# Operand pairs of reused weights stored to HBM at their first use and loaded at their second

## The chip, the cores and the metric

The kernel runs on one core of one Trainium2 chip, in one launch. The metric is the device time of one execution in microseconds; three runs of the kernel before gave 1142.05, 1142.27 and 1142.57, median 1142.27. The engines are TensorE (PE in the profile, its weight loads PEld), VectorE (DVE), ScalarE (ACT), GpSimd (POOL) and SyncE (SP), which issues all of this kernel's DMA transfers on one queue (SPq), in a fixed order.

## The reference

One layer on 1024 tokens of width 1024, float32. In the cut below, `u @ w_in` is the input projection (1024 x 2568), `mix @ w_out` the output projection (1024 x 1024); between them lie a pooling group (p) and a gated delta rule over chunks with q, k, v, z.

```python
u = rms_norm(h, norm_mix[l])
proj = u @ w_in[l]
pool_out = pool_mixer(proj[..., :P], w_pool[l], pool_scale[l])
qkv = causal_conv_silu(proj[..., P:P + 3 * G], conv_w[l])
z = proj[..., P + 3 * G:P + 4 * G]
...
gdn_out = gated_delta_net(qkv[..., :G], qkv[..., G:2 * G], qkv[..., 2 * G:], z, a, b, ...)
mix = jnp.concatenate([pool_out, gdn_out], axis=-1)
h = h + mix @ w_out[l]
u = rms_norm(h, norm_mlp[l])
h = h + jnp.square(jax.nn.relu(u @ w_up[l])) @ w_down[l]
return rms_norm(h, norm_final)
```

## The kernel before

**Pairs.** Matrix products keep float32 accuracy by splitting each operand into a rounded part (hi, type float32r) and the rest (lo) and adding three products: hi x hi, hi x lo, lo x hi (`mm3`, `mm3_steps`). `split_w` makes a weight's pair: SyncE loads the raw block into one of three `raw` buffers (line 128), ScalarE casts it to hi (line 132), and VectorE or GpSimd subtracts to get lo (line 133). The pairs live in the pool `ws` under the tags `wh` and `wl`, five buffers each: a sixth pair waits until the first one's last matmul is through.

**Input projection.** The 1024 tokens are taken as two halves of 512 (i = 0 and 1). `project(i, what, eng)` makes 512 output columns for one half in two blocks of 256 columns; `in_weights(col, eng)` makes a block's four pairs of [128, 2, 256] (256 KB a part). A block is 48 matmuls: first pairs 0 and 1 for both groups of 128 columns, then pairs 2 and 3 for both. The first half goes k, q, v, z, p; the second k, q, v, p, z. So each of the ten blocks of weights is loaded and split twice, once for each half. `eng`, which subtracts, is GpSimd for k of the first half and VectorE for the rest of it, and GpSimd for all of the second half.

**Strands.** Between the matmuls of the projections run the steps of the delta rule (`prepare`, `query`, `invert`, `correct`, `scan`), the gates, the convolutions and the pooling, as generators. `dense()` and `run()` put TensorE's instructions in one order, worked out from TensorE's own assumed rate, and this order is kept as written. The order on the other engines and on SyncE's queue is made by a scheduler from its own simulated times, with earlier lines of the program first among what is ready; only in part of the MLP is VectorE's and ScalarE's order written out too.

**Output projection.** `wout_weights(n, ks)` makes the eight pairs of [128, 512] for columns half n; pairs 4 to 7 lie in a pool `wo`, which opens where the projection's inputs u were. `out_proj(t, n, wt, ...)` adds one tile of 128 tokens: 24 matmuls over the eight pairs in order k = 0 to 7. Tiles 0 to 3 take both halves; tiles 4 to 7 first take half 1, and then, after the recurrence has ended and the MLP's inputs for the first tokens have been transposed (`turn_first`), half 0, for which the eight pairs of half 0 are loaded and split a second time (lines 880 and 881), pairs 4 to 7 with raw buffers of their own (pool `w2`).

**MLP.** Up and down projection follow from about 475 us on. Nothing in them is touched.

Of the kernel before, what the change touches and what calls it, by code (L numbers as in the profile page):

```python
# [8 lines left out]
F32 = mybir.dt.float32  # L9
F32R = mybir.dt.float32r  # L10
# [5 lines left out]
P = 128  # L16
# [3 lines left out]
KT = D // P  # L20
NT = S // P
NH = 4
HALF = 512
# [5 lines left out]
def hybrid_trunk(ctx, tc, x, norm_mix, w_in, conv_w, w_pool, pool_scale, a_log, dt_bias,  # L29
                 gdn_norm, w_out, norm_mlp, w_up, w_down, norm_final, out):  # L30
    nc = tc.nc
    V, A, G, T = nc.vector, nc.scalar, nc.gpsimd, nc.tensor
# [23 lines left out]
    def opened(**kw):  # L56
        c = tc.tile_pool(**kw)
        return c, c.__enter__()

    def close(c):  # L60
        c.__exit__(None, None, None)

    const = ctx.enter_context(tc.tile_pool(name="const", bufs=1))
    ws = ctx.enter_context(tc.tile_pool(name="ws", bufs=2))
# [6 lines left out]
    def big_tile(nm, shape, dt=F32):  # L71
        return big.tile([P] + shape, dt, name=nm, tag="big")
# [4 lines left out]
    def load_x(i):  # L77
        xin[i] = []
        for j in range(2):
            t = big_tile("xin", [2, D])  # L80
            for e in range(2):
                r0 = (CH * i + 2 * j + e) * P
                nc.sync.dma_start(out=t[:, e, :], in_=x2[r0:r0 + P, :])
            xin[i].append(t)
# [40 lines left out]
    def split_w(src, shape, eng, hp=None, ht="wh", lt="wl", bufs=5, rp=None, rbufs=3):  # L125

        raw = (rp or ws).tile(shape, F32, name="raw", tag="raw", bufs=rbufs)
        last["load"] = nc.sync.dma_start(out=raw, in_=src)
        hp = hp or ws
        hi = hp.tile(shape, F32R, name=ht, tag=ht, bufs=bufs)  # L130
        lo = hp.tile(shape, F32R, name=lt, tag=lt, bufs=bufs)
        A.copy(hi, raw)  # L132
        eng.tensor_tensor(lo, raw, hi.bitcast(F32), op=ALU.subtract)  # L133
        return hi, lo
# [7 lines left out]
    def mm3_steps(acc, wh, wl, mh, ml, first, last):  # L142
        T.matmul(acc, wh, mh, start=first, stop=False)
        yield
        T.matmul(acc, wh, ml, start=False, stop=False)
        yield
        T.matmul(acc, wl, mh, start=False, stop=last)
        yield
# [51 lines left out]

    wv = w_in2.rearrange("(k p) c -> p k c", p=P)

    def in_weights(col, eng):
        return [split_w(wv[:, 2 * b:2 * b + 2, col:col + 256], [P, 2, 256], eng) for b in range(4)]

    first_weights = in_weights(512 + 512, G)

# [43 lines left out]
    for l in range(7):  # L251
        b = 1 << l
        m = gp.tile([P, P], F16, name=f"lev{l}")
# [33 lines left out]
    def start(g):  # L287
        strands.append([g, T.now])
# [207 lines left out]
    def bank():  # L496
        return work_bank().rearrange("p (h c) -> p h c", h=NH)
# [242 lines left out]
    wov = w_out2.rearrange("(k p) n -> p k n", p=P)  # L740
    ht, pools = [], {}

    def load_h(i):
        for j in range(2):
            t = big_tile("h", [2, D])
            for e in range(2):
                r0 = (CH * i + 2 * j + e) * P
                nc.sync.dma_start(out=t[:, e, :], in_=x2[r0:r0 + P, :])
            ht.extend([t[:, 0, :], t[:, 1, :]])

    def wout_weights(n, ks):

        return [split_w(wov[:, k, n * HALF:(n + 1) * HALF], [P, HALF], V,
                        *((pools["wo"], "woh", "wol", 4) if k >= 4 else ())) for k in ks]
# [6 lines left out]
    def out_split(t):  # L761
        i, cs = t // CH, (t % CH) * P
        mh = pools["mo"].tile([P, KT, P], F32R, name="mh", tag="mh")
        ml = pools["mo"].tile([P, KT, P], F32R, name="ml", tag="ml")
        for o, src in ((0, pT), (4, qT)):
            A.copy(mh[:, o:o + 4, :], src[i][:, :, cs:cs + P])
            V.tensor_tensor(ml[:, o:o + 4, :], src[i][:, :, cs:cs + P], mh[:, o:o + 4, :], op=ALU.subtract)
        return mh, ml

    def out_proj(t, n, wt, bank, parts=None):  # L770
        mh, ml = parts or out_split(t)
        acc = bank()
        for k in range(KT):
            wh, wl = wt[k]
            yield from mm3_steps(acc, mh[:, k, :], ml[:, k, :], wh, wl, k == 0, k == KT - 1)
        hsl = ht[t][:, n * HALF:(n + 1) * HALF]
        V.tensor_tensor(hsl, acc, hsl, op=ALU.add)

    def gated(ts):

        for t in ts:
            yield f"o{t}"
            gate_out(t)
            yield 1.0
            done(f"g{t}", 0.5)

    wt = {}

    def late_cols():
        yield 4.0  # L790
        turn_rows(rows, cols)
        V.tensor_scalar(gnorm, cols[:, 52:53], 0.5, None, op0=ALU.mult)
# [8 lines left out]
    def dense():  # L801
        start(late_cols())
        yield from project(0, "k", G)
        start(gates(0, *u[0], gts))
        for strand in (scans, corrects, inverts, prepares, queries):
            start(strand())
        yield from project(0, "q", V)
        yield from project(0, "v", V)
        load_x(1)
        yield from project(0, "z", V)  # L810
        start(second_u(norm_u(1)))
        yield from project(0, "p", V)
        yield from project(1, "k", G)
        start(gates(1, *u[1], gts))
        yield from project(1, "q", G)
        yield from project(1, "v", G)
        yield from project(1, "p", G)
        yield from project(1, "z", G, conv_done)
        yield "g0"
        parts = out_split(0)  # L820
        wt[0] = wout_weights(0, range(4))
        close(upc)
        pools["woc"], pools["wo"] = opened(name="wo", bufs=2)
        wt[0] += wout_weights(0, range(4, KT))
        load_h(0)
        for n in range(2):
            if n:
                wt[1] = wout_weights(1, range(KT))
            for t in range(CH):
                if not n:  # L830
                    yield f"g{t}"
                yield from out_proj(t, n, wt[n], acc_bank, parts)
                parts = None
        load_h(1)
        start(gated(range(CH, NT - 1)))
        for t in range(CH, NT - 1):
            yield f"g{t}"
            yield from out_proj(t, 1, wt[1], acc_bank)
# [14 lines left out]
    parts = out_split(NT - 1)  # L853
# [3 lines left out]
    wpc, wp = opened(name="wp", bufs=5, side="right", reuse_waits="tile")  # L857
# [2 lines left out]
    for i in (1, 2):  # L860
        TH[i], TL[i] = (u2p.tile(ub, F32R, name=f"t{m}{i}") for m in "hl")
    R = {21: u2p.tile(ub, F32, name="r21", tag="r21"), 11: big_tile("r11", [4, HALF])}
    w2c, w2p = opened(name="w2", bufs=4, side="right", reuse_waits="tile")

    def whole(g):
        for _ in g:
# [2 lines left out]
    def turn_first(xs):  # L869

        for k in range(KT):
# [5 lines left out]

    turn_first(xs)
    whole(out_proj(NT - 1, 1, wt[1], acc_bank, parts))
    wt[0] = [split_w(wov[:, k, :HALF], [P, HALF], V, *((wp, "wh", "wl", 5, w2p, 6) if k >= 4 else (None, "wh", "wl", 5)))  # L880
             for k in range(KT)]
    whole(out_proj(4, 0, wt[0], work_bank))
    whole(out_proj(5, 0, wt[0], work_bank))
    ys = norm_v(1, 0)
# [1 line left out]
    whole(out_proj(7, 0, wt[0], work_bank))  # L886
    close(pools["moc"])
    close(pools["woc"])
    close(w2c)
    u3c, u3p = opened(name="u3", bufs=1, side="right", reuse_waits="tile")  # L890
    u3 = lambda nm, dt: u3p.tile(ub, dt, name=nm, tag="u3", bufs=6)
    TH[3], TL[3], TH[6], TL[6] = (u3(nm, F32R) for nm in ("th3", "tl3", "th6", "tl6"))
# [221 lines left out]
    kept, raw_x, raw_w = [], {}, {}  # L1114
# [137 lines left out]
```

## Time and profile before

| what | value |
|---|---|
| median of 3 runs | 1142.27 us |
| profiled execution, its own time | 1142.87 us |
| its span | 1140.8 us |
| TensorE busy | 1091.9 us, 96% |
| VectorE busy | 762.5 us, 67% |
| ScalarE busy | 599.9 us, 53% |
| GpSimd busy | 257.1 us, 23% |
| HBM read, written | 121.18 MB, 33.55 MB |

Times in the profile count from the start of the span. Busy time of TensorE has modelled ends, since matmuls overlap: two of them that follow each other closely count as one stretch. Idle time of an engine in front of an instruction is put down to what released it, written as `[idle <-engine tile line]`. Many instructions have the line of a helper (44 and 48 are TensorE's).

### The profile page before, as it was taken

How to read it: one execution, taken by the hardware profiler on the slowest of the kernel's cores; microseconds unless marked ns; L12 is line 12 of the kernel's file. 1: busy time of each engine (PE TensorE's matmuls, PEld its weight loads, DVE VectorE, ACT ScalarE, POOL GpSimd, SP SyncE). 2: the span in 40 equal slices, each digit the busy share in tenths (PEclk: the TensorE clock that was granted, in tenths of full speed). 3: DMA queues.
4: the chain of work that ended last, by engine and by line, in shares of the span. 5: the costliest groups of instructions: out<-in, count | busy, mean ns of one | idle time of the engine just before them, and what ended most of it. 6: DMA issues, size and time to landing. Idle time of an engine off the chain costs nothing.

```text
span 1140.8 us, 15548 instructions
## 1 busy us (share of the span) xinstructions
PE 1091.9 (96%) x5606; PEld 890.2 (78%) x5606; DVE 762.5 (67%) x1240; ACT 599.9 (53%) x1113; POOL 257.1 (23%) x239
## 2 busy tenths in 40 slices
PE   6999999989999899997999999999899999999997
PEld 5787887767778688785778888888788878888885
DVE  5797598778887665668665656564545687476584
ACT  6667566575666464654545455554533333334363
POOL 7023144263551301022423131322000000000020
PEclk9999999999999999999999999999999999999999
DMA  5233211112223221120644444443596895355561
GB/s 164 84 104 119 74 52 51 47 47 56 60 58 129 93 75 37 56 79 26 227 152 154 148 156 148 151 153 112 205 385 229 307 361 198 104 192 188 199 203 74
DMA packets 94359, 155.76 MB, mean 137 GB/s; under 512 B 8069, under 2 KB 47050, under 8 KB 94282
## 3 DMA queue, kind: packets, MB, share of 16 engines
q1 hardware_dynamic: 94282, 154.76, 40.2%
q8 instruction: 44, 0.72, 0.3%
q14 instruction: 33, 0.27, 0.1%
HBM read 121.18 MB, written 33.55 MB: 136 GB/s over the span
## 4 chain that ended last, share of the span: by engine, by line
PE 68%; DVE 11%; ACT 3%; POOL 2%; DMA 2%; issue 2%; POOLq 0%; SPq 0%; DVEq 0%; ACTq 0%
PE bank L44 51%; PE acc L44 17%; DVE cy L396 2%; DMA x<-hd 1%; DVE tl L919 1%; PE bank L48 1%; DVE wl L959 1%; DVE r L914 1%; POOL rk L152 1%; DMA wu<-in_w_up_dram 0%; DMA w<-in_w_down_dram 0%; POOL wu L993 0%; DVE xx L595 0%; ACT wh L958 0%; POOL wl L133 0%
## 5 line engine op out<-in xcount | busy, mean ns | idle before, releaser
L44 PE MATMUL bank<-th,wh 128*128 128x512 f32 x448 | 176.5, 394 | 8.1 <-DVE v L1049 4.3
L44 PE MATMUL bank<-th,wl 128*128 128x512 f32 x448 | 176.5, 394 | 1.0 <-DVE wl L959 1.0
L44 PE MATMUL bank<-tl,wh 128*128 128x512 f32 x448 | 176.5, 394 | 0.0
L958 ACT CAST sh<-x 128x1024 fp32r<-128x1024 f32 x55 | 57.9, 1053 | 157.4 <-PE bank L44 157.3
L44 PE MATMUL bank<-th,sl 128*128 128x512 f32 x344 | 133.8, 389 | 0.0
L44 PE MATMUL bank<-th,sh 128*128 128x512 f32 x344 | 133.8, 389 | 0.0
L44 PE MATMUL bank<-tl,sh 128*128 128x512 f32 x344 | 133.8, 389 | 0.0
L44 PE MATMUL acc<-uh,wh 128*128 128x512 f32 x320 | 129.6, 405 | 1.0 <-DVE ul L173 0.7
L958 ACT CAST wh<-wu 128x512 fp32r<-128x512 f32 x110 | 67.4, 621 | 118.1 <-PE bank L44 102.1
L44 PE MATMUL acc<-ul,wh 128*128 128x512 f32 x320 | 128.5, 402 | 0.0
L44 PE MATMUL acc<-uh,wl 128*128 128x512 f32 x320 | 128.0, 400 | 0.0
L959 DVE TENSOR_TENSOR sl<-x,sh 128x1024 fp32r<-128x1024 f32 x55 | 67.3, 1223 | 84.4 <-ACT sh L958 84.4
L959 DVE TENSOR_TENSOR wl<-wu,wh 128x512 fp32r<-128x512 f32 x110 | 83.3, 763 | 37.0 <-ACT wh L958 36.1
L44 PEld LDWEIGHTS bank<-th,wh 128*128 128x128 f32 x448 | 84.8, 189 | 28.6 <-issue 6.1
L44 PEld LDWEIGHTS bank<-th,wl 128*128 128x128 f32 x448 | 84.8, 189 | 20.8 <-DVE wl L959 2.3
L44 PEld LDWEIGHTS bank<-tl,wh 128*128 128x128 f32 x448 | 84.8, 189 | 18.4
L133 POOL TENSOR_TENSOR wl<-raw,wh 128x512 fp32r<-128x512 f32 x48 | 66.9, 1397 | 92.9 <-ACT wh L132 88.6
L152 POOL TENSOR_TENSOR stf<-stf,mhalf 128x1 f32<-128x1 f32 x8 | 7.9, 999 | 328.5 <-DVE stf L1185 328.5
L44 PEld LDWEIGHTS bank<-tl,sh 128*128 128x128 f32 x344 | 64.6, 188 | 13.5
L44 PEld LDWEIGHTS bank<-th,sh 128*128 128x128 f32 x344 | 64.6, 188 | 13.5
L44 PEld LDWEIGHTS bank<-th,sl 128*128 128x128 f32 x344 | 64.6, 188 | 13.2
L44 PEld LDWEIGHTS acc<-uh,wh 128*128 128x128 f32 x320 | 60.3, 188 | 12.9 <-ACT cy L394 1.3
(319 smaller groups left out, 2284.6 us busy)
## 6 DMA issues: line engine op xcount, KB each, us to landing
w<-in_w_down_dram SPq DMA_DIRECT2D x56, 512.0 KB, 6.0
x<-hd SPq DMA_DIRECT2D x56, 512.0 KB, 3.3
raw<-in_w_in_dram SPq DMA_DIRECT2D x80, 256.0 KB, 2.7
wu<-in_w_up_dram SPq DMA_DIRECT2D x16, 1024.0 KB, 7.7
hd<-s SPq DMA_DIRECT2D x48, 256.0 KB, 2.1
w<-in_w_down_dram SPq DMA_DIRECT2D x32, 256.0 KB, 7.3
raw<-in_w_out_dram SPq DMA_DIRECT2D x24, 256.0 KB, 2.6
xin<-in_x_dram SPq DMA_DIRECT2D x8, 512.0 KB, 4.7
```

What stands on the lines that cost most here:

```text
L44: T0.matmul(out, lhsT, rhs, start=start, stop=stop, skip_group_check=goes_on)
L48: T0.transpose(out, in_, identity)
L133: eng.tensor_tensor(lo, raw, hi.bitcast(F32), op=ALU.subtract)
L152: last["rsqrt"] = G.tensor_tensor(s, s, mhalf[:, :n], op=ALU.pow)
L396: V.scalar_tensor_tensor(cy, cr[:, e:e + HALF], tap[e], cy, op0=ALU.mult, op1=ALU.add)
L914: V.scalar_tensor_tensor(r, turned_banks[k], nmlp[:, k:k + 1], x, op0=ALU.mult, op1=ALU.subtract)
L919: V.tensor_tensor(TL[i][:, j, :], src[j], TH[i][:, j, :].bitcast(F32), op=ALU.subtract)
L958: A.copy(hi, src)
L959: V.tensor_tensor(lo, src, hi.bitcast(F32), op=ALU.subtract)
```

## The change

`in_weights` keeps what it has made: at a block's first use the four pairs are split as before, and `keep_parts` then stores hi and lo of each pair to tiles in HBM (eight stores of 256 KB a block, on SyncE's queue). At the second use `load_parts` loads both parts back, straight into `wh` and `wl` buffers. The same is done with the eight pairs of half 0 of the output projection, whose second use loads 16 parts, pairs 4 to 7 first, in place of splitting; `out_proj` then goes through them in that order. The pool `w2` is gone.

```diff
+    wdp = ctx.enter_context(tc.tile_pool(name="wd", bufs=1, space=bass.MemoryType.DRAM))
+    in_parts = {}
+
+    def keep_parts(nm, pairs):
+
+        kept = []
+        for b, parts in enumerate(pairs):
+            to = [wdp.tile(m.shape, F32, name=f"{nm}{b}{e}") for m, e in zip(parts, "hl")]
+            for d, m in zip(to, parts):
+                nc.sync.dma_start(out=d, in_=m.bitcast(F32))
+            kept.append(to)
+        return kept
+
+    def load_parts(kept, pool=None):
+        parts = []
+        for m, tag in zip(kept, ("wh", "wl")):
+            t = (pool or ws).tile(m.shape, F32R, name=tag, tag=tag, bufs=5)
+            nc.sync.dma_start(out=t.bitcast(F32), in_=m)
+            parts.append(t)
+        return parts
+
     def in_weights(col, eng):
-        return [split_w(wv[:, 2 * b:2 * b + 2, col:col + 256], [P, 2, 256], eng) for b in range(4)]
+        if col in in_parts:
+            return [load_parts(kept) for kept in in_parts[col]]
+        wt = [split_w(wv[:, 2 * b:2 * b + 2, col:col + 256], [P, 2, 256], eng) for b in range(4)]
+        in_parts[col] = keep_parts(f"wd{col}_", wt)
+        return wt
...
     def out_proj(t, n, wt, bank, parts=None):
         mh, ml = parts or out_split(t)
         acc = bank()
-        for k in range(KT):
+        ks = list(wt if isinstance(wt, dict) else range(KT))
+        for k in ks:
             wh, wl = wt[k]
-            yield from mm3_steps(acc, mh[:, k, :], ml[:, k, :], wh, wl, k == 0, k == KT - 1)
+            yield from mm3_steps(acc, mh[:, k, :], ml[:, k, :], wh, wl, k == ks[0], k == ks[-1])
...
-    wt = {}
+    wt, wo_parts = {}, []
...
         wt[0] += wout_weights(0, range(4, KT))
+        wo_parts.extend(keep_parts("wdo", wt[0]))
         load_h(0)
...
-    w2c, w2p = opened(name="w2", bufs=4, side="right", reuse_waits="tile")
...
-    wt[0] = [split_w(wov[:, k, :HALF], [P, HALF], V, *((wp, "wh", "wl", 5, w2p, 6) if k >= 4 else (None, "wh", "wl", 5)))
-             for k in range(KT)]
+
+    wt[0] = {k: load_parts(wo_parts[k], wp if k >= 4 else ws) for k in (4, 5, 6, 7, 0, 1, 2, 3)}
...
-    close(w2c)
```

## Rows read from the trace of the kernel before

**Rows 1.** Busy time by stretch: start:end, length, engines (instructions), clock, DMA share, GB/s.
```profile
15.00:205.00 190.00, 184.04 (x1105) 148.26 (x1105) 146.98 (x320) 124.64 (x279) 65.94 (x76) 1.00 0.29 83
205.00:352.00 147.00, 138.45 (x930) 111.38 (x929) 117.58 (x225) 95.64 (x227) 67.50 (x49) 1.00 0.23 68
352.00:460.00 108.00, 104.96 (x664) 86.37 (x664) 67.43 (x136) 54.07 (x120) 17.01 (x16) 0.98 0.19 64
460.00:475.00 15.00, 13.46 (x77) 11.04 (x76) 11.78 (x18) 13.59 (x25) 1.29 (x1) 1.00 0.26 82
```

**Rows 2.** Order of time on TensorE: start, duration, instruction, idle before and releaser.
```profile
238.52 0.38 PE L44 MATMUL bank<-xx,tt 128*128 128x128 f16 x4 [1.53 <-ACT qT L397]
...
257.71 0.40 PE L44 MATMUL bank<-tt,ee 128*128 128x128 f16 x4 [0.84 <-DVE ee L617]
...
291.26 0.63 PE L48 MATMUL bank<-ident,kn 128*128 128x128 f32 x4 [1.28 <-DVE kn L538]
...
303.92 0.40 PE L44 MATMUL bank<-tt,ee 128*128 128x128 f16 x4 [0.77 <-DVE ee L617]
...
342.71 0.38 PE L44 MATMUL bank<-xx,tt 128*128 128x128 f16 x4 [0.81 <-DVE xx L595]
...
466.08 0.50 PE L44 MATMUL acc<-wh,mh 128*128 128x512 f32 x1 [1.08 <-ACT r L876]
...
471.65 0.39 PE L44 MATMUL bank<-wh,mh 128*128 128x512 f32 x1
...
473.20 0.50 PE L44 MATMUL bank<-wl,mh 128*128 128x512 f32 x1 [0.46 <-DVE wl L133]
```

**Rows 3.** Order of time on VectorE and GpSimd ahead of four of these stops.
```profile
233.73 4.13 DVE L396 SCALAR_TENSOR_TENSOR cy<-cr,cols,cy 128x512 f32<-128x512 f32 x3
...
288.13 1.29 POOL L133 TENSOR_TENSOR wl<-raw,wh 128x512 fp32r<-128x512 f32 x1
...
289.39 1.01 POOL L152 TENSOR_TENSOR rk<-rk,mhalf 128x4 f32<-128x4 f32 x1
...
301.69 2.70 POOL L133 TENSOR_TENSOR wl<-raw,wh 128x512 fp32r<-128x512 f32 x2
301.76 1.50 DVE L555 TENSOR_TENSOR m<-m,ident_h 128x512 f16<-128x512 f16 x1
...
340.11 1.32 POOL L133 TENSOR_TENSOR wl<-raw,wh 128x512 fp32r<-128x512 f32 x1 [3.26 <-ACT wh L132]
...
340.31 1.15 DVE L414 COPY nxt<-nxt 128x8 f32<-128x8 f32 x1
```

**Rows 4.** Two lines by source: least, median and most ns; first, last start.
```profile
L396 DVE SCALAR_TENSOR_TENSOR cy<-cr,cols,cy x72: 734/746/1868, 27.4 to 300.0; 128x512 f32<-128x512 f32 x72
...
L555 DVE TENSOR_TENSOR m<-m,ident_h x8: 398/416/1504, 79.0 to 393.7; 128x512 f16<-128x512 f16 x8
```

**Rows 5.** Busy time in 205 to 352: weight subtractions, then casts (us, instructions).
```profile
205.00:352.00 147.00, 0.00 (x0) 39.57 (x29) 1.00 0.23 68
...
205.00:352.00 147.00, 17.84 (x29) 1.00 0.23 68
```

**Rows 6.** DMA issues in 205:352 and 475:820: count, size, us to landing.
```profile
raw<-in_w_in_dram SPq DMA_DIRECT2D x27, 256.0 KB, 2.7
...
hd<-s SPq DMA_DIRECT2D x45, 256.0 KB, 2.1
```

**Rows 7.** Order of time on SyncE's queue: first start, duration, count.
```profile
321.55 3.97 SPq L426 DMA_DIRECT2D wr<-in_w_pool_dram  x2
...
352.74 18.56 SPq L128 DMA_DIRECT2D raw<-in_w_out_dram  x5
...
460.74 1.75 SPq L128 DMA_DIRECT2D raw<-in_w_out_dram  x4
```

**Rows 8.** Order of time on ScalarE at the start, as rows 2.
```profile
20.66 1.38 ACT L132 CAST wh<-raw 128x512 fp32r<-128x512 f32 x2 [1.14 <-DMA raw<-in_w_in_dram]
```

**Rows 9.** TensorE's waits in 370 to 390: us in total, times, longest.
```profile
PE acc L44 <- DVE wol L133: 3.0, 2, 1.9
```

## The prediction, as it was put on record

> **What bounds the kernel now.** I read the busy time of each engine by stretch first, then TensorE's stops in order of time, then what ran on the other engines ahead of each stop. The stretches are: first use of the input weights (15 to 205 us, the projections of the first 512 tokens), second use (205 to 352), first use of the output weights (352 to 460), second use (460 to 475); the MLP follows. In these four TensorE is busy 184.04 of 190, 138.45 of 147, 104.96 of 108 and 13.46 of 15 us [rows 1]. So TensorE sets the time, in an order written out by hand, and what an edit elsewhere can give back is the idle rest: 5.96, 8.55, 3.04 and 1.54 us. The MLP has idle time too, but no touched instruction runs there.
>
> The idle time of the second use is made of short stops. The five that matter here are 1.53, 0.84, 1.28, 0.77 and 0.81 us, all of a recurrence step on TensorE behind a VectorE or ScalarE result [rows 2]. The order of time ahead of each shows why the result is late [rows 3]. At 301.69 GpSimd starts two weight subtractions (2.70 us together), and the VectorE instruction of 301.76 beside them takes 1.50 us, against a median of 0.416 for its line [rows 4]; the same picture stands ahead of the stop at 257.71 (an instruction of the same form, 1.51 us). At 289.39 GpSimd's reciprocal root starts only when the subtraction of 288.13 is through. The small copy of 340.31 takes 1.15 us beside the subtraction of 340.11. The three convolution steps of 233.73 take 4.13 us, where three times their median of 0.746 is 2.24 [rows 3, 4].
>
> **The change, part by part.** *Second use of the input weights, what goes.* Forty pairs are no longer made: 40 loads of 256 KB, 40 casts on ScalarE, 40 subtractions on GpSimd. In the 147 us of this stretch that is 29 subtractions, 39.57 us of GpSimd, and 29 casts, 17.84 us of ScalarE or 0.62 each [rows 5]. None of it is TensorE's time, so it is worth only what it takes out of the stops. At 257.71 the stretched step loses 1.51 - 0.416 = 1.09, more than the stop, so all 0.84 goes; at 303.92 the same, 0.77; at 291.26 the root can start up to 1.29 earlier, so all 1.28 goes; at 342.71 the copy shrinks, and I take the whole 0.81; at 238.52 the excess of 1.89 is shared with GpSimd work of the recurrence that stays, so I take half of 1.53, 0.77. Sum 0.84 + 0.77 + 1.28 + 0.81 + 0.77 = 4.47 us. The upper end is 8.55, all idle time of the stretch. The lower end is a loss of the same 4.47: the planner gives VectorE, ScalarE and GpSimd a new order, and a late result can be made later as well as earlier. I take 4.47, because for four of the five a weight subtraction stands at the cause and the fifth is counted half. Late next is what makes up the other 4.1 us, stops with no subtraction ahead of them.
>
> The Trainium skill speaks against counting every stop. "SBUF — State Buffer", section "Who interferes with whom", says that a VectorE instruction with two SBUF inputs contends with a GpSimd instruction that reads SBUF, and one with at most one SBUF input does not, outside the two-port modes. The stretched instructions of 301.76 and 233.73 have two SBUF inputs, and there the trace agrees (1.50 against 0.416); the copy of 340.31 has one, and its 1.15 us fits only the exception. By the rule without the exception the stop of 342.71 stays and the sum would be 3.66 in place of 4.47.
>
> *Second use, what comes.* 80 loads of 256 KB go straight into the operand tiles. The trace has no such load; nearest are the raw load of the same bytes, 2.7 us to landing, and the hidden-layer store of 256 KB, 2.1 us [rows 6]. Each waits until TensorE has let go of the tile five pairs back. A block of 256 columns is 48 matmuls; by the loop order its first pair is last used at the 18th, and the pair that takes over its tile is first used at the 55th, 36 matmuls on. From 466.08 to 471.65 there are 24 matmuls [rows 2], 0.232 us each, so 36 are 8.4 us, and the recurrence in between makes it longer. From release to use it takes two issues of SyncE at 1.75 / 4 = 0.44 [rows 7] and a landing, 2 x 0.44 + 2.7 = 3.6 us. So the loads are hidden with 4.8 us to spare: 0. The cover gone is the slower rival below. On SyncE's queue behind such a load stand the next pairs, the pool weights, the residual and the output weights; the strands and the output projection wait for those.
>
> *First use.* 80 stores of 256 KB are new, at 0.44 us of issue 35 us of SyncE's 190. Their 21 MB add 110 GB/s to the 83 now, at which the DMA engines are busy 0.29 of the time [rows 1]; in proportion that becomes 0.68, not full. Each store waits for its cast or its subtraction, and what stands behind it on SyncE (the next raw loads, pool weights, the second x) waits too. The raw buffers run three pairs ahead of the five operand pairs, and that lead hides it: 0, with 2 us as the loss without the lead and no gain possible. A tile is held until its store has read it (2.1 us), but TensorE holds it longer. The one place without lead is the start, where ScalarE already waits 1.14 us for a raw load at 20.66 [rows 8]: eight stores of the first block ahead of the second block's loads would add 8 x 0.44 = 3.5 us of issue. Between 0 and 3.5 I take 0.5, near to 0, since those loads' buffers come free before the last stores can go.
>
> *Output weights.* The first use gains 16 stores behind casts and subtractions that stay. Its two stops on a subtraction, 3.0 us [rows 9], can move either way with VectorE's new order: 0, ends -3.0 and +3.0. In the second use 8 casts, 8 subtractions and 8 loads go and 16 loads come. TensorE stops 1.08 us at 466.08 for a ScalarE copy and 0.46 at 473.20 for a subtraction [rows 2]; ScalarE is busy 13.59 of 15 us there [rows 1]. One cast less ahead of that copy is worth 0.62, and the 0.46 goes whole: 1.08 together, ends 0 and 1.54. The loads of the upper four pairs can go at 460.74 at the latest, where SyncE issues their raw loads now [rows 7]: 8 x 0.44 + 2.7 makes 467.0, ahead of 471.65. The turned order (4 to 7, then 0 to 3) gives the lower four twelve matmuls more. The dropped pool of raw buffers hid nothing that was waited for.
>
> **Sum.** -4.47 + 0.5 + 0 - 1.08 = -5.05 us. The profiled execution took 1142.87 us (a span of 1140.8 and 2.07 around it), which gives 1137.8; the median of the runs is 0.60 below that execution, so 1137.2 us.
>
> **Rivals.** *The stops come back.* VectorE stays 80% busy in the second use (117.58 of 147 [rows 1]), and the next late result may stand right behind each stop that goes. For it: the five are five different results, and another 4.1 us of stops lie between them. Against: two are one stretched instruction and nothing else. Then only the output part and the start are left: 1142.27 - 1.08 + 0.5 = 1141.7. If the change did not take the work off the engines at all, it would look the same.
>
> *SyncE becomes the wait (the slower side).* In the second use every operand tile hangs on one queue of fixed order, with no raw buffers in front. An entry that waits holds all pairs behind it: two pool weights held it 3.97 us at 321.55, five output weights 18.56 us at 352.74 [rows 7]. What a hold has over 4.8 us stops TensorE. Two holds of 10 us (pool projection, last projection) are 2 x 5.2 = 10.4, so 1137.2 + 10.4 = 1147.6; the kernel is measurably slower from 5.05 + 2.3 = 7.4 us of such stops on. For it: the 18.56 is there now. Against: that entry waits for raw buffers, which are free in the changed kernel.
>
> *More than the named stops.* The lighter engines empty all 8.55 us, and the stops of the first output use (3.0) go too, since VectorE comes to them with less behind it: 1142.27 - 8.55 - 3.0 - 1.08 + 0.5 = 1130.1.
>
> **Chances and range.** Forecast 0.48, the stops come back 0.22, SyncE 0.16, more 0.14. A measurement of this kernel tells a change from none at about 0.2%, 2.3 us: faster is below 1140.0, slower above 1144.6. The forecast and the larger gain are faster, 0.62; same 0.22; slower 0.16. The forecast's own range is 1134 to 1140 (half of its bounds, 2 to 3 us either way); the one that leaves out 2 in 10 reaches into the larger gain down to 1131.5 and into the SyncE case up to 1145.
>
> **What would show it.** In the second use no weight subtraction on GpSimd and no weight cast; the two-input VectorE lines near their medians; TensorE idle about 4 us where it was 8.55; no stop like those of 257.71, 291.26 and 303.92, and none like 473.20; no new stop before 30 us. It is wrong if TensorE waits for a load of an operand tile, if idle time in the first use grows by over 2 us, or if the time stays although those stops are gone.

## The result and the profile after

The changed kernel took 1135.1 us (median of 6 runs, 1130.0 to 1136.7) beside 1142.4 us of the kernel before (6 runs, 1139.8 to 1143.5): a ratio of 0.9929, interval 0.9918 to 0.9940, so 7 to 9 us faster. The forecast of 1137.2 us lies 2.1 us above the median. The direction held, and the range of 1134 to 1140 us held this median; x12, the same kernel again, came out at 1133.7 us, just under it. The terms of the sum did not hold, as the profile shows. Ratios are of runs in the fast state: four of x3's six runs (1158 to 1162 us) and one of the kernel before beside x5 to x8 (1362 us) fell in a slower one and are left out. The profiled execution is the one with the least time of the six, 1130.04 us (span 1128.3), 12.83 us below the profiled one of before.

The same stretches by engine, in the columns of [rows 1]. Each begins and ends at about the same TensorE instruction as there; since the work now ends sooner, the limits are 11 us earlier from the end of the second on:

```profile
15.00:205.00 190.00, 183.83 (x1109) 148.50 (x1108) 146.06 (x321) 120.04 (x270) 50.47 (x65) 1.00 0.63 206
205.00:341.00 136.00, 135.78 (x929) 110.80 (x928) 98.72 (x222) 80.89 (x198) 25.15 (x20) 1.00 0.39 126
341.00:449.00 108.00, 104.87 (x658) 85.68 (x658) 65.83 (x135) 53.21 (x119) 16.31 (x15) 0.97 0.33 112
449.00:464.00 15.00, 14.44 (x82) 12.17 (x81) 9.07 (x14) 12.29 (x22) 1.28 (x1) 1.00 0.60 193
```

The second use of the input weights (second line) holds as many TensorE instructions as before, 929 against 930, in 136 us in place of 147, and TensorE is idle for 0.22 us of it where it was 8.55. GpSimd's busy time there fell from 67.50 to 25.15 us, VectorE's from 117.58 to 98.72 although the change takes none of its instructions there (222 in the window against 225). The first use (first line) is idle for 6.17 us, where it was 5.96. The share of the DMA engines in it rose from 0.29 to 0.63.

TensorE in order of time. The first line is the only stop left in the second use; the next five are the instructions that stood behind the five stops of [rows 2], in the same order; the last two answer to 466.08 and 471.65 there:

```profile
230.66 0.38 PE L44 MATMUL bank<-xx,tt 128*128 128x128 f16 x4 [0.22 <-DVE xx L621]
...
236.03 0.40 PE L44 MATMUL bank<-xx,tt 128*128 128x128 f16 x4
...
252.46 0.40 PE L44 MATMUL bank<-tt,ee 128*128 128x128 f16 x4
...
283.55 0.60 PE L48 MATMUL bank<-ident,kn 128*128 128x128 f32 x4
...
295.03 0.40 PE L44 MATMUL bank<-tt,ee 128*128 128x128 f16 x4
...
332.21 0.40 PE L44 MATMUL bank<-xx,tt 128*128 128x128 f16 x4
...
455.87 0.50 PE L44 MATMUL acc<-wh,mh 128*128 128x512 f32 x1 [0.56 <-ACT r L903]
...
461.44 0.40 PE L44 MATMUL bank<-wh,mh 128*128 128x512 f32 x1
```

No bracket stands behind the five: none is waited for. Ahead of them on VectorE and GpSimd, as in [rows 3]: three convolution steps take 2.32 us and not 4.13, the mask product 0.41 and not 1.50, and GpSimd's root stands behind no subtraction. The small copy that took 1.15 us takes 0.17 (329.38).

```profile
231.74 2.32 DVE L422 SCALAR_TENSOR_TENSOR cy<-cr,cols,cy 128x512 f32<-128x512 f32 x3
```
```profile
279.80 1.01 POOL L152 TENSOR_TENSOR rk<-rk,mhalf 128x4 f32<-128x4 f32 x1
```
```profile
293.52 0.41 DVE L581 TENSOR_TENSOR m<-m,ident_h 128x512 f16<-128x512 f16 x1
```

**Where the time went, instruction by instruction.** TensorE runs the same 5606 matmuls in the same order in all these kernels, so each can be compared with itself. The table gives the start of the same matmul minus its start in the profiled execution before (us), at six points of that execution; the column behind them is the second use, 205 to 352, which is 146.83 us before; then the profiled execution's whole difference and the median of the kernel's runs. It is worked out from the start times of the traces.

```
                       40      80     205     352     400     480   second use   whole   median
changed kernel        0.35    2.46   -0.25  -10.97   -9.78  -10.95    136.12    -12.83   1135.1
x12 (the same again)  3.33    3.77    1.04   -9.67   -8.49   -9.65    136.12    -11.59   1133.7
x1  GpSimd's work     3.94    5.86    6.24    5.01    6.08    4.92    145.60      3.15   1145.7
x2  ScalarE's work    3.88    4.30    1.30   -7.46   -5.40   -6.66    138.08     -8.26   1136.6
x8  GpSimd fills      0.10    6.27    3.26   -5.74   -3.76   -5.02    137.84     -6.19   1134.4
x5  input part        2.60    3.36    0.66  -10.06  -11.62  -11.50    136.12    -12.96   1133.4
x6  output part       0.09    0.16    0.13    0.10    1.37    0.19    146.80     -1.28   1141.6
x4  k not stored     -0.33    1.93    0.69  -10.01   -7.95   -9.19    136.12     -9.26   1132.6
x9  low parts only   -0.81    2.03   -0.45  -10.19   -8.28   -9.53    137.09    -10.76   1132.2
x10 ScalarE's queue  -0.64    3.05   -0.66  -11.35   -9.26  -10.49    136.14    -10.67   1132.0
x11 x9, no k, input  -0.06    0.08   -0.70  -10.49   -9.65   -9.65    137.04     -8.87   1133.5
x7  8 of 80 stores   -0.62    1.12   -2.26  -12.96  -11.12  -12.38    136.12    -13.69   1129.3
```

For the changed kernel: 2.5 us lost in the first 80 us, 2.7 won back by 205, 10.7 won in the second use, 1.2 lost at the first use of the output weights, 1.2 won at the second. The last 1.9 us come behind 480 us, 1.6 of them in the MLP and 0.3 outside the span. No changed instruction runs there, and the kernel x6, which is level with before at 480 us, gains 1.5 there too. Of it 1.4 (x6: 1.0) come between 822 and 830 us, where TensorE's granted clock was 0.58 in the profiled execution of before, 0.79 in x6 and 0.79 in the changed kernel (811 to 819 there). So most of that part belongs to the profiled execution of before, not to the change.

### The profile page after: what moved, and what is told of

Its sections match the earlier page's. It is cut to its first block, busy times and chain, and to the rows that moved or that the text cites. A ratio compares the mean times of both kernels' runs of the same rounds, so it can differ in the third digit from the quotient of the medians.

```text
span 1128.3 us, 15667 instructions
## 1 busy us (share of the span) xinstructions
PE 1086.9 (96%) x5606; PEld 887.5 (79%) x5606; DVE 737.0 (65%) x1232; ACT 575.5 (51%) x1065; POOL 198.4 (18%) x199
## 4 chain that ended last, share of the span: by engine, by line
PE 76%; DVE 6%; ACT 3%; DMA 2%; issue 1%; POOL 1%; POOLq 0%; SPq 0%; DVEq 0%; ACTq 0%
PE bank L44 52%; PE acc L44 22%; PE bank L48 1%; DMA w<-in_w_down_dram 1%; DVE tl L945 1%; DVE wl L985 1%; DVE r L940 1%; DMA wu<-in_w_up_dram 0%; POOL wu L1019 0%; ACT wh L984 0%; DVE tl L985 0%; ACT junk L536 0%; POOL wu L1011 0%; DVE kept L1166 0%; DVE xx L621 0%
## 5 line engine op out<-in xcount | busy, mean ns | idle before, releaser
L44 PEld LDWEIGHTS acc<-uh,wl 128*128 128x128 f32 x320 | 60.3, 188 | 10.7
L44 PEld LDWEIGHTS acc<-ul,wh 128*128 128x128 f32 x320 | 60.3, 189 | 10.2
```

The source lines that it names most:

```text
L44: T0.matmul(out, lhsT, rhs, start=start, stop=stop, skip_group_check=goes_on)
```

## The experiments

**Whose work was in the way (x1, x2, x3, x8).** Theory: the second use was long because GpSimd's subtractions read SBUF beside VectorE's two-input instructions. Rivals: GpSimd's own recurrence steps queued behind the subtractions; ScalarE's casts were in the way.

x1 keeps the loads and lets GpSimd subtract again:

```diff
-            return [load_parts(kept) for kept in in_parts[col]]
+            for kept in in_parts[col]:
+                hi, lo = load_parts(kept)
+                junk = ws.tile([P, 2, 256], F32R, name="junk_w", tag="raw", bufs=3)
+                G.tensor_tensor(junk, hi.bitcast(F32), lo.bitcast(F32), op=ALU.subtract)
```

> The changed kernel, but at each of the 40 second uses GpSimd also subtracts the two loaded parts into an unused buffer: the same 128x512 subtraction as before the change (about 1.3 us each, 40 of them, two SBUF inputs), on a result nobody needs. The load, the saved casts and everything else stay. Theory A (the gain of the second use is GpSimd's work taken away, through VectorE's stretched instructions and GpSimd's own queue): the second use, which went from 147 to about 136 us in the profiles, gives back 6 to 11 us, so the time is 1141 to 1144, little below the kernel before. Theory B (it is ScalarE's 25 us of casts): at most 2 us come back, about 1136. Theory C (it is the new order of the planner or the raw buffers that went): near 1135 as the changed kernel.

Measured: 1145.67 us, ratio 1.0020 (1.0007 to 1.0033), above the range expected: its trace loses 5.9 us by 80 us, against 2.5 in the changed kernel. The second use takes 145.60 us, so 9.5 of its 10.7 us are lost again, though loads and stores are all as in the changed kernel.

x2 gives ScalarE a cast for each second use in the same place (`A.copy(junk, hi.bitcast(F32))`).

> The changed kernel, but at each of the 40 second uses ScalarE also copies the loaded high part into an unused buffer: the same 128x512 cast as before the change (about 0.62 us each). Theory A (GpSimd): 0 to 3 us come back, 1135 to 1138. Theory B (ScalarE): 6 to 11 us come back, 1141 to 1144. Theory C: near 1135.

Measured: 1136.56 us, ratio 0.9933 (0.9920 to 0.9947). The second use takes 138.08 us: the casts carried 2.0 us at most.

x3 was to hold GpSimd with four memsets for each second use.

> The changed kernel, but at each of the 40 second uses GpSimd fills an unused buffer with zeros in four steps, some 1.3 us together as estimated from the 0.21 us of a 128x128 fill: it holds GpSimd's queue, but reads no SBUF. Two forms of theory A are told apart. If the second use lost by GpSimd's own queue (the reciprocal roots and other recurrence steps late behind a subtraction), this gives back about as much as the subtraction does, 5 us or more, 1140 or above. If it lost by VectorE instructions with two SBUF inputs that stand beside a reading GpSimd, this gives back under a third of it: 1135 to 1138, and the VectorE lines that were stretched stay near their medians.

A miss: the memsets waited for nothing, and in the profiled execution all 160 ran from 144.6 to 220.7 us, ahead of the second use, which begins at 233.5 there. Measured: 1133.1 and 1137.6 us, ratio 0.9926 (0.9906 to 0.9947). It says nothing of the second use. x8 ties them down:

```diff
+                here = G.tensor_tensor(junk[:, 0, 0:1], hi.bitcast(F32)[:, 0, 0:1], lo.bitcast(F32)[:, 0, 0:1], op=ALU.add)
+                with tc.issue_after(here.ins):
+                    for e in range(4):
+                        G.memset(junk[:, e % 2, :], 0.0)
```

> As the changed kernel, but at each of the 40 second uses GpSimd adds one element a partition of the two loaded parts and then fills the unused buffer with four memsets of 128x256 (about 4 x 0.31 us), which read nothing of SBUF; its result isn't used. GpSimd is then held in the second use about as long as by the subtractions of the kernel before. If the second use was long because VectorE and GpSimd contend when both read SBUF: VectorE's instructions stay at their means of the changed kernel (copy of the column 0.80 us, mask product 0.41 us), the second use stays at 136 to 139 us and the time at 1134 to 1138 us. If it was long because GpSimd's other work queued behind its subtractions, or because any GpSimd instruction slows VectorE: 1140 us or more.

Measured: 1134.37 us, ratio 0.9925 (0.9910 to 0.9940); the second use takes 137.84 us. The costliest groups on VectorE and GpSimd in the second use tell the three apart (shape and count, busy us, mean ns, idle before them). Before:

```profile
L396 DVE SCALAR_TENSOR_TENSOR cy<-cr,cols,cy 128x512 f32<-128x512 f32 x30 | 29.3, 977 | 4.0 <-ACT cy L394 3.6
...
L555 DVE TENSOR_TENSOR m<-m,ident_h 128x512 f16<-128x512 f16 x4 | 3.8, 956 | 1.3 <-POOL m L554 1.3
```

The changed kernel:

```profile
L422 DVE SCALAR_TENSOR_TENSOR cy<-cr,cols,cy 128x512 f32<-128x512 f32 x30 | 23.8, 795 | 4.3 <-ACT cy L420 3.9
```

x1:

```profile
L428 DVE SCALAR_TENSOR_TENSOR cy<-cr,cols,cy 128x512 f32<-128x512 f32 x31 | 31.3, 1010 | 3.7 <-ACT cy L426 3.2
...
L587 DVE TENSOR_TENSOR m<-m,ident_h 128x512 f16<-128x512 f16 x4 | 3.8, 958 | 1.3 <-POOL m L586 1.3
...
L231 POOL TENSOR_TENSOR junk_w<-wh,wl 128x512 fp32r<-128x512 f32 x30 | 41.8, 1398 | 45.4 <-DMA wl<-wd_1l 19.1 <-DMA wl<-wd_3l 15.1 <-DMA wl<-wd_0l 7.3
```

x8:

```profile
L431 DVE SCALAR_TENSOR_TENSOR cy<-cr,cols,cy 128x512 f32<-128x512 f32 x30 | 25.1, 835 | 4.5 <-ACT cy L429 4.1
...
L234 POOL MEMSET junk_w<- 128x256 f32 x118 | 31.8, 310 | 0.0
L231 POOL TENSOR_TENSOR junk_w<-wh,wl 128x1 f32<-128x1 f32 x29 | 7.7, 265 | 47.7 <-DMA wl<-wd_1l 22.6 <-DMA wl<-wd_3l 13.1 <-DMA wl<-wd_0l 9.9
```

GpSimd is held as long in x8 (31.8 + 7.7 = 39.5 us) as in x1 (41.8), but VectorE's convolution step means 835 ns, near the 795 without that work, and not 1010. So the time of GpSimd is not what counts but that it reads SBUF: of the 9.5 us that x1 gives back, holding GpSimd alone gives back 137.84 - 136.12 = 1.7. Nor is it that one memset is shorter than a subtraction. By their starts and ends, seven of x8's convolution steps run beside memsets and no other GpSimd work: six take 735 to 752 ns and one 832. In x1 the five that begin with 1 us and more of a subtraction still to run take 1.55 to 1.81 us. The three steps of over 1.5 us that x8 has left run beside GpSimd's own recurrence work on two inputs. Small copies differ: the 128x3 copies into `cr` mean 478 ns before, 226 in the changed kernel and 492 in x8, so fills stretch them as reads do. GpSimd and VectorE in x8, a copy and then a convolution step, each beside four memsets:

```profile
257.25 1.07 POOL L234 MEMSET junk_w<- 128x256 f32 x4
...
259.50 1.07 POOL L234 MEMSET junk_w<- 128x256 f32 x4
```
```profile
257.44 0.90 DVE L423 COPY cr<-chalo 128x3 f32<-128x3 f32 x1
...
260.04 0.73 DVE L431 SCALAR_TENSOR_TENSOR cy<-cr,cols,cy 128x512 f32<-128x512 f32 x1
```

Those 1.7 us are one stop, and it shows the queue: in x8 GpSimd's root starts only when three memsets are through, VectorE's step behind it is late, and TensorE stops for 1.54 us.

```profile
244.71 0.83 POOL L234 MEMSET junk_w<- 128x256 f32 x3
245.51 1.00 POOL L152 TENSOR_TENSOR rk<-rk,mhalf 128x4 f32<-128x4 f32 x1
```
```profile
247.38 0.63 PE L48 MATMUL bank<-ident,kn 128*128 128x128 f32 x4 [1.54 <-DVE kn L573]
```

Before, TensorE stopped at the same matmul for 1.46 us, but not by the queue: GpSimd was idle for 2.09 us ahead of this root, waiting for VectorE, and VectorE had come late out of two convolution steps, the first of them beside a subtraction (2.36 us together, where twice the median is 1.49). GpSimd, VectorE and TensorE before:

```profile
240.72 1.29 POOL L133 TENSOR_TENSOR wl<-raw,wh 128x512 fp32r<-128x512 f32 x1
244.10 1.44 POOL L152 TENSOR_TENSOR rk<-rk,mhalf 128x4 f32<-128x4 f32 x1 [2.09 <-DVE rk L535]
```
```profile
240.98 2.36 DVE L396 SCALAR_TENSOR_TENSOR cy<-cr,cols,cy 128x512 f32<-128x512 f32 x2 [1.37 <-ACT cy L394]
```
```profile
246.41 0.63 PE L48 MATMUL bank<-ident,kn 128*128 128x128 f32 x4 [1.46 <-DVE kn L538]
```

The Trainium skill ("SBUF — State Buffer", section "Who interferes with whom") says that a VectorE instruction with two SBUF inputs contends with a GpSimd instruction that reads SBUF, not with one that only writes it. x1 and x8 agree: the convolution steps mean 1010 ns with the reads and 835 with the fills.

**The two halves (x5, x6).** x5 leaves the output projection as before, x6 the input weights.

```diff
 # x5
-        wo_parts.extend(keep_parts("wdo", wt[0]))
-    wt[0] = {k: load_parts(wo_parts[k], wp if k >= 4 else ws) for k in (4, 5, 6, 7, 0, 1, 2, 3)}
+    wt[0] = [split_w(wov[:, k, :HALF], [P, HALF], V, ...) for k in range(KT)]
 # x6
-        if col in in_parts:
-            return [load_parts(kept) for kept in in_parts[col]]
-        in_parts[col] = keep_parts(f"wd{col}_", wt)
```

> The input part of the change alone; the output projection's half is split at both uses, as before. The theory (the second use of the input weights carries the whole gain, and the output part gives back at its first use, 369 to 376 us, about what it gains at 466 to 473 us, 1.24 us): the time is within 1 us of the changed kernel's, so 1134 to 1137 us, and the ratio to the kernel before 0.992 to 0.994. If the output part were worth its own 1.24 us and the wait at its first use were only the clock, 1136.3 us. If it cost on balance (the 1.9 and 1.1 us waits at 369 to 376 us come from its stores): 1133 to 1134 us.

Measured: 1133.41 us, ratio 0.9925 (0.9912 to 0.9938).

> The output part of the change alone; the input weights are split at both uses, as before. Its own gain at 466 to 473 us is 1.24 us in the changed kernel's trace. The theory: 1.2 us faster at 466 to 473 us, up to 1.2 us lost at 369 to 376 us, so 1142.4 to 1144 us beside a kernel before of 1143 to 1144, ratio 0.999 to 1.000. The rival, that the two parts help each other and the gain in the second use of the input weights needs both: the two halves' ratios then don't multiply to 0.993.

Measured: 1141.59 us, ratio 0.9991 (0.9982 to 0.9999). By that interval the output part is worth 2 us at most. The table shows why: x6 is level with before up to 380 us, loses 1.26 by 400 and wins 1.2 by 480. In the changed kernel TensorE waits at the first output use for a subtraction as before ([rows 9]) and then for a cast instead of a second subtraction:

```profile
PE acc L44 <- DVE wol L133: 1.9, 1, 1.9
PE acc L44 <- ACT woh L132: 1.0, 1, 1.0
```

The waits are 2.9 us in place of 3.0, but TensorE then runs longer at the lower clock. In the windows of 4 us (start:end, length, TensorE busy, granted clock, DMA share, GB/s) the lowest granted clock of the changed kernel is 0.50, all of it at 1.2 GHz:

```profile
368.00:372.00 4.00, 1.76 (x7) 0.66 1.02 376
372.00:376.00 4.00, 3.86 (x9) 0.50 0.87 312
```

and that of before is 0.71:

```profile
380.00:384.00 4.00, 2.76 (x11) 0.86 0.33 105
384.00:388.00 4.00, 4.00 (x22) 0.71 0.27 95
```

The DMA engines, at 1.02 in place of 0.33, are carrying the last of the 16 new stores there. In x5, without these stores, TensorE waits 3.0 us as before, the granted clock stays at 1.00 from 360 to 380 us, and 1.6 us are won from 352 to 400 us (table).

**What the stores cost (x7, x4, x9, x10, x11).** In the median the changed kernel gains 7.3 us and in the profiles 11.6 to 12.8, and the table shows 2.5 to 6.3 us lost by 80 us wherever all the parts are stored (the first five rows and x5). Theory: the stores cost this, at the start. x7 stores only the first block of columns.

```diff
-        in_parts[col] = keep_parts(f"wd{col}_", wt)
+        in_parts[col] = in_parts.get(1024) or keep_parts(f"wd{col}_", wt)
```

> As the changed kernel, but only the first block of columns stores its parts (8 of the 80 stores); every second use loads from these 8, so as many loads stay, and the values of the second use are not the right ones. It prices the other 72 stores. Theory (the stores fill the DMA engines to 0.8 to 0.9 at 20 to 50 us, the raw words land in 3.5 instead of 2.7 us, and ScalarE's casts wait for them): the start's loss, 2 to 5 us by 80 us of the span, falls to under 1 us, and the time is 1131 to 1134 us. Rival (the loss at the start is the order of the instructions or the clock, not the stores): the time stays at 1135 to 1137 us, and the loss by 80 us is as in the changed kernel.

Measured: 1129.26 us, ratio 0.9880 (0.9867 to 0.9893), faster than expected: by the medians the 72 stores cost 0.5%, 5 to 6 us. By the profiled executions, which for the changed kernel are its fastest runs, it is 0.9 and 2.1. x4 leaves out k's two blocks, which come first in the span:

```diff
-        in_parts[col] = keep_parts(f"wd{col}_", wt)
+        if col not in (1024, 1280):
+            in_parts[col] = keep_parts(f"wd{col}_", wt)
```

> The changed kernel, but the two blocks of k (the first weights of all) are neither stored nor loaded: they are split twice as before the change; 64 stores stay in place of 80 for the input weights. In the changed kernel TensorE came 2.0 to 2.5 us later out of the stretch 40 to 60 us than before, where the DMA engines were busy 0.9 of the time and ScalarE waited for raw loads. If the stores of the first blocks crowd those raw loads, that loss goes (TensorE at the gates' matmuls as early as before, 52.2 us) and at most 1.5 us of the second use is lost again with eight subtractions: 1133 to 1135.5. If the loss comes from the order on ScalarE and not from the transfers, the time stays or rises: 1135 to 1138.

Measured: 1132.58 us, ratio 0.9901 (0.9889 to 0.9914), below the changed kernel's interval: storing k's blocks costs more than their second use gives. x12 is the changed kernel again.

> The changed kernel itself once more, for a second profile: the first one is of its fastest run, 1130.0 us, 5 us under the median of its runs. If the loss at the start is what differs from run to run (the profiles of kernels with all stores on SyncE show ScalarE's copy abT at 45.7 to 47.7 us, the kernel before at 43.0), a run near the median shows it at 46.5 to 47.5 us and a loss of 3.5 to 5 us by 80 us of the span, with the second use of the input weights again at 136 us; the median is 1134 to 1136 us. If the start is as in the first profile, the difference lies behind 475 us, in the part that the change doesn't touch. It gives the comparison with the kernels that store less a second ratio.

Measured: 1133.71 us (1131.3 to 1137.3), ratio 0.9932 (0.9917 to 0.9946). The profile fell again on the run with the least time (1131.28 us), so one of 1135 us and more has no trace. But this one shows how the loss arises, three steps in a row. SyncE's queue at the start (first start, duration, count):

```profile
20.45 0.41 SPq L213 DMA_DIRECT2D wd_3h<-wh  x1
24.09 0.34 SPq L213 DMA_DIRECT2D wd_0h<-wh  x1
24.82 0.32 SPq L213 DMA_DIRECT2D wd_1h<-wh  x1
25.23 0.41 SPq L213 DMA_DIRECT2D wd_3l<-wl  x1
25.69 1.00 SPq L128 DMA_DIRECT2D raw<-in_w_in_dram  x2
```

The store of 24.09 waits until ScalarE has cast its part (23.44, below), and the raw loads behind it go at 25.69; before, the first of them went at 22.5. ScalarE waits 4.26 us for it:

```profile
23.44 1.35 ACT L132 CAST wh<-raw 128x512 fp32r<-128x512 f32 x2 [2.99 <-DMA raw<-in_w_in_dram]
...
30.12 0.62 ACT L132 CAST wh<-raw 128x512 fp32r<-128x512 f32 x1 [4.26 <-DMA raw<-in_w_in_dram]
```

The convolution steps behind that cast come late, TensorE stops, and the granted clock falls to 0.60 in the next 4 us (1.00 there before, last line), so for most of them the chip gave 1.2 GHz:

```profile
31.87 0.50 PE L44 MATMUL acc<-uh,wh 128*128 128x512 f32 x1 [2.48 <-ACT cy L420]
```
```profile
28.00:32.00 4.00, 1.52 (x8) 1.00 0.58 191
32.00:36.00 4.00, 4.00 (x12) 0.60 0.97 301
```
```profile
32.00:36.00 4.00, 4.00 (x20) 1.00 0.43 130
```

Twelve matmuls fit in those 4 us where 20 did. A stop of 2.5 us so costs 4.4: TensorE's lead over before goes from 1.08 us at 30 us to a lag of 3.33 at 36. Not every run pays it. In the first trace of the changed kernel the loads go as late (25.73), but the cast behind them starts at 28.78 and not 30.12, and TensorE does not stop there; of the seven traces with all these stores on SyncE four have a stop of 1.9 to 3.0 us at this matmul (x12, x1, x2, x5). x9 and x10 take the wait for casts off SyncE, in two ways.

```diff
 # x9: only the low parts are stored; the high parts are cast again at the second use
-        in_parts[col] = keep_parts(f"wd{col}_", wt)
+        in_parts[col] = keep_parts(f"wd{col}_", [(lo,) for _, lo in wt])
+                nc.sync.dma_start(out=raw, in_=wv[:, 2 * b:2 * b + 2, col:col + 256])
+                nc.sync.dma_start(out=lo.bitcast(F32), in_=kept)
+                A.copy(hi, raw)
 # x10: all are stored, the high parts from ScalarE's queue
-            for d, m in zip(to, parts):
-                nc.sync.dma_start(out=d, in_=m.bitcast(F32))
+            for d, m, q in zip(to, parts, (nc.scalar, nc.sync)):
+                q.dma_start(out=d, in_=m.bitcast(F32))
```

> As the changed kernel, but of the input weights only the low parts are stored (40 of the 80 stores go); at the second use the words are loaded again, ScalarE casts them to the high parts as before, and the low parts are loaded. GpSimd's subtractions stay away from the second use. Theory (the stores cost some 5 us: the run with 72 of them gone is 0.5% faster than the changed kernel): half of the stores gone gives about half back, 2 to 4 us, 1131 to 1133 us, and the second use stays at 136 to 138 us. If SyncE's waits for the cast high parts ahead of the next words are the whole price (27.8 us of SyncE's waits by 100 us), nearly all comes back: 1129 to 1131 us. If ScalarE's 40 casts cost at the second use: 1135 us or more.

Measured: 1132.15 us, ratio 0.9904 (0.9890 to 0.9919).

> As the changed kernel, with as many stores, but the high parts' stores are issued by ScalarE, which wrote them, and not by SyncE; SyncE waits for no cast ahead of the loads of words. It tells the two prices of the stores apart. Theory A (the loads of words queue on SyncE behind stores that wait for casts): the loads start earlier, the loss by 80 us of the span goes from 2 to 5 us to about 1 us as without stores, 1130 to 1133 us. Theory B (the DMA engines' share, 0.77 at 15 to 60 us with or without): the time stays at 1134 to 1137 us. ScalarE's issues, some 0.05 to 0.4 us each by 44, can add up to 4 us if they lie on the path of its casts: over 1137 us would show that.

Measured: 1132.01 us, ratio 0.9898 (0.9882 to 0.9915). Either saves about half of what x7 saves. At 40 us both stand at -0.6 to -0.8 in the table: the stop at 32 us is gone. x10 moves as many bytes, but no store that waits for a cast stands ahead of its raw load, which goes at 22.69, as before the change, so that one was SyncE's queue, not the bytes:

```profile
22.69 3.15 SPq L128 DMA_DIRECT2D raw<-in_w_in_dram  x2
```

The other half stays: both lose 3.6 to 3.7 us between 44 and 48 us, where TensorE stops 1.9 and 2.0 us for ScalarE's copy abT and the granted clock falls (0.86 and 0.71 in x9's windows from 44 to 52). That copy starts at 42.98 us before, 42.97 in x7, 43.77 in x4, 44.89 in x9, 45.19 in x10, 45.74 and 46.63 in the two traces of the changed kernel. What goes along with it is how long a raw load takes to land while the DMA engines are fuller (their share and the loads' median in 15 to 60 us):

```
before 0.36, 2.8 us    x7 0.46, 2.7    x4 0.59, 3.0    x9 0.59, 3.1    x10 0.76, 3.9    changed 0.77, 3.9
```

So the loads are longer by up to 1.1 us where more bytes are stored. That this alone makes abT late is not shown: x4 and x9 have the same share and nearly the same landing, and their abT is 1.1 us apart. One more piece stays open: the stop behind g_hi at 52 to 56 us, 0.64 us before, is 1.25 in x7 and 1.4 in x4 and the changed kernel, with and without stores. In x7 the granted clock falls behind it, and all that x7 loses by 80 us is lost there (-0.62 at 50 us, 1.12 at 58):

```profile
52.20 0.25 PE L44 MATMUL bank<-g_hi,u_r 128*128 128x16 f32 x1 [1.25 <-DVE g_hi L387]
```
```profile
52.00:56.00 4.00, 3.80 (x16) 0.77 0.23 66
56.00:60.00 4.00, 4.00 (x16) 0.81 0.36 79
```

x11 joins x9 with x4 and x5:

> The candidate: only the low parts are stored, only of the eight blocks of columns other than k's two, and the output projection's half is split at both uses as before. If each saving holds beside the others (not storing k: 2 to 3 us; low parts alone: 2 to 3 us; output part: about 0): 1129 to 1132 us, at or under the kernel that doesn't store k (1132.6). If the stores cost only in the first 60 us, where k's are, the low parts alone add nothing to that: 1132 to 1133 us.

Measured: 1133.50 us, ratio 0.9916 (0.9901 to 0.9930). It loses nothing at the start (0.08 at 80 us, abT at 43.05), but from 180 to 205 us it wins 0.7 where x9 and x10 win 2.4 and 2.8, at k's second use, and in the profile behind 480 us it loses 0.8 where the others win 0.1 to 1.9. The savings don't add up. Leaving x7 aside, x4, x9 and x10 are the fastest, 1132 us, some 11 us below before, and the runs can't tell them apart.

## Why the prediction was right, and where its sum was wrong

*The second use of the input weights* carried the gain, and through the mechanism that was put first: x1 shows that GpSimd's subtractions are nine tenths of it (9.5 of 10.7 us), and x8 that 7.8 of these 9.5 come with their reading of SBUF and not with the time they hold GpSimd. The size was off by more than half: -4.47 predicted, -10.7 measured, past the end of 8.55 that was called all there was. This is the mis-sized term. Two things were missed.

First, "what an edit can give back is the idle rest" is too low. The profile's idle time begins when the last matmul's row ends, and a matmul's row lasts 0.39 us, while matmuls in a row start 0.23 apart. So each stop costs 0.16 more than its bracket says. The shifts of the same instructions show it: the stop of 1.53 gave 1.69, that of 0.84 gave 1.00, that of 0.81 gave 0.97. Twelve stops went and one of 0.22 came, 8.3 us of idle and 11 x 0.16 = 1.8 more: 10.1 of the 10.7. The rest is in shifts of 0.2 us and less that leave no bracket; it stays open.

Second, "stops with no subtraction ahead of them" were to stay, 4.1 us. All but 0.22 us went. The largest (246.41, 1.46 us) did have a subtraction ahead, further back than was looked: it stood beside the convolution step of 240.98, on which VectorE's next steps, the root and this matmul waited in turn. For the smaller ones the cause stays open. Halving the stop of 238.52 was too careful as well; beside GpSimd's recurrence work that stays (25 us) TensorE stops for 0.22 us in all. Taking the whole 0.81 of 342.71 was right, against the sum of 3.66: the copy ahead of it went from 1.15 to 0.17 us, and x8 stretches such copies even by fills.

*The loads of the second use* are hidden, as predicted. SyncE waits often behind a tile that TensorE still holds, up to 10.6 us, and they land in 2.6 to 4.5 us, not 2.7, yet TensorE's only wait in this stretch is the 0.22 above. So the slower rival, in which what a hold on SyncE has over 4.8 us stops TensorE, had its holds and not its price.

*The start* was predicted at +0.5, ends 0 and 3.5, on the ground that the raw buffers "come free before the last stores can go". That failed: the store does stand ahead of the load and waits for a cast (24.09 above). The loss by 80 us was 2.5 and 3.8 in the two traces of the changed kernel and up to 6.3 in others with all stores. The price was not in issue time, as worked out, but in stops, one of which, in x12, takes the clock down with it.

*The first-use stores* were costed at nothing because the DMA share would become 0.68, "not full". It became 0.63, but loads were slower to land well below a full share. x7 prices the stores at 5 to 6 us altogether by the medians. Behind 80 us nothing of it is seen: the first use even wins 2.7 us back by 205, 2.0 of them from 180 on, where k's second use has begun (x1's subtractions start at 155.3) and x4, without it, wins 0.7. So at 205 us the two traces of the changed kernel stand at -0.25 and 1.04, about the 0.5 that was predicted for the whole of the first use, by two errors of opposite sign.

*Output weights*: second use -1.08 predicted, -1.24 measured; first use 0 predicted, +1.2 measured, within its ends. Together nothing in the traces, which x6 confirms (0.19 at 480 us).

That the median came out near the forecast is in part luck. In the two traces the errors do not cancel: these executions took 12.8 and 11.6 us less than the profiled one of before, more than twice the 5.05 of the sum, and the mis-sized second use (6 us too little gain) is most of the difference. But both traces are of the fastest runs; the medians lie 5.1 and 2.4 us higher, and that loss, which no trace shows, brings them back to the forecast. "More than the named stops" was the better account of the second use. Its 1130.1 is the time of the traced run, but its 3.0 us of the first output use did not go (2.9 us of waits are left), so that match is luck too, and its price forgot the stores. What makes the runs between 1130 and 1137 us differ is not shown, since no trace of the changed kernel is from the upper end. It may be the stops at the start, which cost between 2.5 and 6.3 us by 80 us in the table. In keeping with stops that lower the clock, the two longest of x12's six runs (1136.9 and 1137.3 us) have the lowest mean granted clock, 0.986 against 0.987 to 0.991.

## What to carry to other kernels

Work on an engine with time to spare is not free if it reads SBUF beside an engine that feeds the critical one: compare the means of that engine's instructions with their medians before calling the work hidden. Count a TensorE stop as its idle time plus what a matmul's row lasts beyond the pitch. A store in a queue of fixed order makes every load behind it wait for the store's data, so ask first what stands behind it where there is no lead, at the start of the kernel, and store only what pays.

## What the runs showed of the hardware that was not expected

GpSimd held for 39.5 us of a 138 us stretch by memsets cost 1.7 us; held for 41.8 by two-input subtractions, 9.5. Loads of 256 KB went from 2.8 to 3.9 us to landing while the share of the DMA engines went from 0.36 to 0.77. A single stop of 2.48 us at the start was followed by a granted clock of 0.60 over the next 4 us and cost 4.4 us in all; one of 2.54 us in x8 was followed by 0.57:

```profile
44.00:48.00 4.00, 1.46 (x10) 1.00 1.03 344
48.00:52.00 4.00, 4.00 (x12) 0.57 0.20 72
```

The stop of 1.59 us at the same instruction in the changed kernel's first trace left the clock at 1.00:

```profile
46.37 0.42 PE L48 MATMUL bank<-ident,abT 16*128 16x16 f32 x4 [1.59 <-ACT abT L359]
```
```profile
48.00:52.00 4.00, 4.00 (x19) 3.34 (x18) 2.49 (x11) 2.50 (x4) 0.00 (x0) 1.00 0.60 204
```

The length of the one stop does not decide it: behind x7's stop of 1.25 us, shorter than this one, the clock fell (0.77 and 0.81 in the windows above).
